# A two-layer decoder trunk: the convolution's LayerNorm by products with a matrix of ones, and the recurrence's transposes as 64x128 row tiles behind other tiled matmuls

## The chip, the cores and the metric

The kernel runs on one core of a Trainium2 chip. The metric is the device time in microseconds (us) of one execution. The kernel before takes 1475.71 us (median of three runs, 1475.03 to 1475.87).

## What is computed

Two layers work on x (512 tokens, 1024 channels). One projection feeds four branches of width 512: an RWKV-7 recurrence, a latent attention, a gated depthwise convolution and a cross-attention into 256 memory tokens. Each branch is multiplied by its gate and projected to 1024 channels; the four are merged with sigmoid gates, projected once more and normalized.

```python
for l in range(DEPTH):                                   # DEPTH = 2
    h = x @ w_in[l]                                      # all branches' columns
    y_rwkv = _rwkv7_branch(...)                          # 8 heads x 64, state by delta rule
    y_mla  = _mla_branch(...)
    y_conv = _conformer_conv_branch(...)                 # GLU, conv of 31 taps, LayerNorm, swish
    y_mem  = _memory_xattn_branch(...)
    branches = jnp.stack([y_rwkv, y_mla, y_conv, y_mem], axis=2)
    proj  = jnp.einsum('bsnc,ncd->bsnd', branches, w_o_branch[l])
    gates = jax.nn.sigmoid(merge.reshape(B, S, N_BRANCH, D) + b_gate[l])
    x = _layer_norm(DEEPNORM_ALPHA * x + jnp.sum(gates * proj, axis=2) @ w_out[l], ...)
```

## The kernel before, in words

**Large products.** Activations lie with channels on partitions, 512 tokens in a row. Each float32 operand is split into a high and a low part, and a product is made of three matmuls (`mm3`). A projection of 128 channels (`project`: eight blocks of the depth, 24 matmuls of 512 columns) writes a tile `ps_...`; a merge (`merge_items`) makes two such gate tiles `ps_m` and two products `po` of 12 matmuls each with the branch's output projection.

**The order.** `Plan` writes one program order for all engines while the kernel is built. It keeps a clock for each engine with costs that are written in the code, takes the large products from a list of items (`stream`), and steps side tasks (generators, made with `spawn`) as soon as their data should be there. On TensorE it puts a task's matmuls between those of the large products, which so cover the time in which the other engines work on the task. `Plan.shape` charges a change of the array's form (128x128, or tiles of 64x64, 64x128, 128x64). The order is fixed when the program is built; on the chip every engine goes through its own rows in order and waits where data are missing.

**PSUM.** Two banks `pp` hold the large products, two banks `pa` are shared by all side tasks, and the recurrence has two tiles of two banks each (`pg`).

**The convolution.** `taps` adds up the 31 taps of each 128 channels into `cacc` (VectorE). When four are there, `conv_norm` (lines 1288 to 1325) normalizes over the 512 channels of each token. In the kernel before it turns the data on TensorE to have tokens on partitions (`ct`, four transposes for each of four token blocks), takes mean and variance there with `bn_stats`, and turns the result back (`cb`, sixteen more). It starts only when the merge of the cross-attention is complete (line 1290), and turns back only after half of that of the latent attention (line 1311).

**The recurrence.** `rwkv_unit` (lines 838 to 1247) treats two heads' blocks and 256 tokens at once in chunks of 64; a layer has four units. A unit's name ends in layer, first block and half: `_1_2_1` is the last unit of the second layer. In a unit stand in turn: the scores `g` (64x64 tiles, four on the array at once); the substitution, 16x16 triangles inverted on GpSimd with DMA on both sides; `x0` to `x2`, which extend the inverse; `va`; `gb`, the unit's transfer matrices; the chain over the chunks, `w` with the state `S` between its steps; and the output `yb`, which is normalized by head (`bn_stats`, `bn_aggr`, a power on GpSimd in `gr`, eight activations on ScalarE), turned by four transposes `ty` and added into `r`. In the last unit of a layer, `w` is three products with a full array (`Gd`). When a layer's four units are through, `r` times its gate is split (`yrg`), and the layer's last merge, the rows `po0`, can use it; its first two gate tiles, `ps_m00` and `ps_m01`, need no `r`.

The recurrence needs b, k and v with tokens on partitions. The kernel before makes them in `tokens` (lines 1002 to 1013): four full 128x128 transposes `tk0` for b and four `tk1` for k, after the bonus product `bo`, and four `tk2` for v in a task of its own. Each takes one bank of `pa`.

## Time and profile before

| | |
|---|---|
| median of three runs | 1475.71 us |
| the profiled execution: span | 1473.7 us (the runs' median is 2.0 us over it; the time around the span) |
| mean granted TensorE clock | 0.999 |
| TensorE matmul, busy | 1463.7 us, 99% |
| VectorE, busy | 1032.8 us, 70% |
| ScalarE, busy | 681.5 us, 46% |
| GpSimd, busy | 148.3 us, 10% |

In the profile PE is TensorE, DVE VectorE, ACT ScalarE, POOL GpSimd and SP the engine that issues the DMAs. A timeline row has the start in us, the time from its start to the end of the last of its instructions in us, engine, line, operation, the tile written and those read, and how many instructions it stands for; the bracket at its end has the idle time before it and what ended that. A float32 matmul that is no transpose shows as two records. Matmuls overlap, so that the distance from start to start says what one costs.

### The profile page before, as it was taken

The page shows a single profiled execution, that of the slowest core. Times are in us where ns is not written, and L with a number is a line of the kernel's source. Part 1 is how long each engine was busy: PE and PEld are TensorE (multiplying, and loading weights), DVE is VectorE, ACT ScalarE, POOL GpSimd, SP SyncE. Part 2 cuts the span into 40 slices and gives each one's busy share as a digit, 9 for nine tenths or more (in the row PEclk, how much of TensorE's full clock was granted, in tenths as well). Part 3 has the DMA queues.
Part 4 walks back from the last instruction along what each step waited for, and adds up shares of the span by engine and source line. Part 5 has one row for each costly group of instructions (what it writes and reads, how often), then busy time and mean ns, then how long its engine had stood idle before and what let it go on. Part 6 is the DMA issues. An engine that isn't in the chain of part 4 may idle for free.

```text
span 1473.7 us, 28870 instructions
## 1 busy us (share of the span) xinstructions
PE 1463.7 (99%) x11729; PEld 1233.6 (84%) x11729; DVE 1032.8 (70%) x2017; ACT 681.5 (46%) x1325; POOL 148.3 (10%) x339
## 2 busy tenths in 40 slices
PE   9999999999999999999999999999999999999997
PEld 9888888888888888888999888888888888888886
DVE  6799997765657665645554899987867476747756
ACT  5556654425354443443264465633454454444331
POOL 0000000030303030000010000000041203121003
PEclk9999999999999999999999999999999999999999
DMA  7454332232222323334354253333232323233522
GB/s 220 129 144 107 90 110 95 86 77 95 81 77 83 90 76 97 122 122 130 102 166 121 62 151 78 118 94 101 83 96 76 96 57 101 75 86 122 171 96 83
DMA packets 89157, 153.49 MB, mean 104 GB/s; under 512 B 41024, under 2 KB 47424, under 8 KB 89024
## 3 DMA queue, kind: packets, MB, share of 16 engines
q1 hardware_dynamic: 89024, 151.65, 34.9%
q8 instruction: 92, 1.51, 0.4%
q14 instruction: 41, 0.34, 0.1%
HBM read 134.32 MB, written 5.77 MB: 95 GB/s over the span
## 4 chain that ended last, share of the span: by engine, by line
PE 96%; ACT 1%; DMA 1%; DVE 1%; POOL 1%; issue 0%; SPq 0%; DVEq 0%; POOLq 0%
PE ps_m L353 23%; PE po L353 11%; PE pz L353 4%; PE ps_v L353 3%; PE ps_cg L353 3%; PE ps_rg L353 3%; PE ps_xg L353 3%; PE ps_xq L353 3%; PE ps_k L353 3%; PE ps_val L353 3%; PE ps_glu L353 3%; PE ps_r L353 3%; PE ps_mg L353 3%; PE ms L353 2%; PE pl L353 2%; PE x L353 2%
## 5 line engine op out<-in xcount | busy, mean ns | idle before, releaser
L259 DVE SCALAR_TENSOR_TENSOR cacc<-hpad,prm,cacc 128x512 f32<-128x512 f32 x240 | 179.0, 748 | 3.8
L259 ACT ACTIVATE tm<-ps_m,prm 128x512 f32<-128x512 f32 x64 | 44.1, 689 | 152.2 <-PE ps_m L353 149.5
L259 DVE SCALAR_TENSOR_TENSOR mt<-tm,po 128x512 f32<-128x512 f32 x48 | 33.0, 687 | 85.1 <-PE po L353 85.0
L259 POOL TENSOR_TENSOR tmpW<-ZT,W 64x14 f32<-64x14 f32 (+6 forms) x112 | 43.9, 392 | 8.0
L259 ACT ACTIVATE mP<-ms,nmm 128x128 f32<-128x128 f32 (+3 forms) x64 | 33.7, 530 | 20.9 <-DVE nmm L259 16.1
L259 POOL TENSOR_SCALAR ZT<-W 64x256 f32<-64x256 f32 x8 | 4.5, 564 | 361.8 <-DMA W<-scr 361.8
L259 POOL TENSOR_TENSOR ZT<-ZT,tmpW 64x14 f32<-64x14 f32 (+6 forms) x112 | 39.7, 354 | 8.8
L259 DVE TENSOR_TENSOR merged<-merged,mt 128x512 f32<-128x512 f32 x48 | 33.3, 694 | 1.6
L259 POOL MEMSET D<- 128x8 f32 x8 | 0.9, 112 | 328.9 <-PE ms L353 313.0
L259 DVE CUSTOM_DVE_ANT_0 ms<-ms,causal 128x128 f32<-128x128 f32 (+3 forms) x64 | 31.1, 498 | 0.6 <-PE ms L353 0.2
L259 ACT COPY mPT<-mt 128x128 f32<-128x128 f32 (+3 forms) x64 | 26.4, 428 | 5.3 <-PE mt L358 5.0
L259 POOL TENSOR_SCALAR lrs<-lmv 128x1 f32<-128x1 f32 x8 | 4.3, 532 | 231.8 <-DVE lmv L259 226.9
L358 PE MATMUL mt<-cst,mP 128*128 128x128 f32 x160 | 26.8, 274 | 0.4 <-ACT mPT L259 0.4
L259 DVE TENSOR_SCALAR mP<-mP,smm 128x128 f32<-128x128 f32 (+3 forms) x64 | 24.8, 387 | 2.4
L259 DVE SCALAR_TENSOR_TENSOR merged<-tm,po 128x512 f32<-128x512 f32 x16 | 11.0, 687 | 22.0 <-PE po L353 19.9
L358 PEld LDWEIGHTS mt<-cst,mP 128*128 128x128 f32 x160 | 20.2, 140 | 6.8 <-issue 0.9
L259 ACT ACTIVATE yb<-yb,mr,gr 128x64 f32<-128x64 f32 x64 | 22.1, 430 | 1.4 <-DVE mr L259 1.4
L353 PE MATMUL ms<-kTl,qT 96*128 96x128 f32 (+3 forms) x64 | 21.5, 337 | 0.0
L259 POOL TENSOR_SCALAR gr<-gm 128x8 f32<-128x8 f32 x8 | 1.9, 242 | 191.3 <-DVE gm L259 191.3
L353 PE MATMUL ms<-kTh,qTl 96*128 96x128 f32 (+3 forms) x64 | 20.6, 323 | 0.0
L353 PE MATMUL ms<-kTh,qT 96*128 96x128 f32 (+3 forms) x64 | 20.6, 322 | 0.0
L259 ACT ACTIVATE xP<-xs,nmx 128x256 f32<-128x256 f32 x32 | 15.2, 475 | 11.2 <-DVE nmx L259 11.1
(3574 smaller groups left out, 5224.8 us busy)
## 6 DMA issues: line engine op xcount, KB each, us to landing
w<-in_w_ch_dram SPq DMA_DIRECT2D x146, 512.0 KB, 3.7
w<-in_w_o_dram SPq DMA_DIRECT2D x32, 512.0 KB, 3.6
w<-in_w_out_dram SPq DMA_DIRECT2D x16, 512.0 KB, 3.5
w<-in_w_lat_dram SPq DMA_DIRECT2D x15, 336.0 KB, 3.0
w<-in_w_mk_dram SPq DMA_DIRECT2D x8, 512.0 KB, 3.6
w<-in_w_mv_dram SPq DMA_DIRECT2D x8, 512.0 KB, 3.7
w<-in_w_qk_dram SPq DMA_DIRECT2D x8, 320.0 KB, 3.1
mr<-in_memT_dram SPq DMA_DIRECT2D x8, 256.0 KB, 5.6
```

The costliest lines, as they stand in the source:

```text
L259: return self.plan.keep(f(*a, **k))
L353: plan.keep(nc.tensor.matmul(o, lhsT, rhs, start=start, stop=stop))
L358: plan.keep(nc.tensor.transpose(o, i, ident))
```

## The change

**The convolution's norm.** The transposes go. The four `cacc` are added on GpSimd, the sum is split in two, and two matmuls with a 128x128 matrix of ones (`cs`) put the sum over all channels on every partition; the mean is subtracted from `cacc` in place. Squares (ScalarE) are added in the same way and summed by two matmuls (`cq`). One row of this goes by DMA to DRAM and comes back with 512 tokens as 128x4, the power is taken on GpSimd, and two further DMAs bring the result to all partitions. The two conditions on the merges go.

**The transposes of b, k and v.** A transpose is now made of 64 rows by 128 channels (`TQ`, a 64x128 row tile), with the upper and the lower half in different banks, so that two `pa` banks are taken at once. Those of b and k (16) stand directly behind `g`, those of v (8) directly behind the matmuls of `x0`. The inner order of the last group of `x0` changes with it (`for cp, h, c2 in quads`), and a few tiles take other places in SBUF.

```diff
+    def TQ(o, i, one):
+        plan.shape(64, 128)
+        plan.op("PE", 28.0, _names(o), _names(i))
+        plan.keep(nc.tensor.transpose(o, i, one))
...
+            def turned_by(ps, c, src):
+
+                for s in SUB:
+                    for cp in range(2):
+                        for h in range(2):
+                            e = c + 128 * s + 64 * cp
+                            TQ(ps[h][:, e:e + 64], src[s][HALF[h], 128 * cp:128 * cp + 128], one[h])
...
+            tk = yield from pa.take([128, 512], "tk0" + t, 2, None)
+            turned_by(tk, 0, [bt[:, s] for s in SUB])
+            turned_by(tk, 256, [kt[:, s] for s in SUB])
...
-                        TR(ps[:, 256 * s + 128 * cp:256 * s + 128 * cp + 128], src[s][:, 128 * cp:128 * cp + 128])
...
+            tv = yield from pa.take([128, 512], "tk2" + t, 2, None)
...
-                for cp, c2, h in quads:
+                for cp, h, c2 in quads:
                     MM(y0[HALF[h ^ cp], 1, s, h, c2], AR[HALF[h], s, 2 * cp + c2, 0], one[h], start=True, stop=True, four=True)
+            turned_by(tv, 0, vr)
...
-            yield lambda: added[3] == 8
-            for tb in range(4):
...
-                    TR(ps[:, 128 * i:128 * i + 128], cacc[i][:, 128 * tb:128 * tb + 128])
...
-                    TR(ps[:, 128 * tb:128 * tb + 128], ntok[tb][:, 128 * i:128 * i + 128])
...
+            MM(ps, all_ones, lo, start=True, stop=False)
+            MM(ps, all_ones, h, start=False, stop=True)
...
+                V.scalar_tensor_tensor(out=cacc[i], in0=ps, scalar=-1.0 / 512, in1=cacc[i], op0=ALU.mult, op1=ALU.add)
...
+            DMA(d4, row)
...
+            DMA(v4, d4.rearrange("o (p a) -> (o p) a", p=128))
...
+            DMA(d.rearrange("o (p a) -> (o p) a", p=128), v4)
...
+            DMA(rstd, d.to_broadcast([128, 512]))
```

**What moves on TensorE.** With other costs and conditions, `Plan` writes another order. Two places in the last unit of the second layer are shown; a row has the line, the operation, the tile written and those read (names end in layer, unit and a serial number), the size, and how often it stands there. The first place is the chain over the chunks (`w0` to `w2`, with `ps_rg` a projection for the recurrence's gate and `ty_1_2_0` the transposes of the unit before). Before:

```order
L353 MATMUL w0_1_2_1_15086<-S3_1_2_0_14861,Gd0_1_2_1_14850 128x64
L353 MATMUL w0_1_2_1_15086<-S3_1_2_0_14861,Gd1_1_2_1_14851 128x64
L353 MATMUL ps_rg1_1_15074<-xl2_1_8395,w215h_14792 128x512
L353 MATMUL ps_rg1_1_15074<-xh2_1_8394,w215h_14792 128x512
L353 MATMUL ps_rg1_1_15074<-xh2_1_8394,w215l_14793 128x512
L353 MATMUL ps_rg1_1_15074<-xl3_1_8400,w215h_14792 128x512
L353 MATMUL ps_rg1_1_15074<-xh3_1_8399,w215h_14792 128x512
L353 MATMUL ps_rg1_1_15074<-xh3_1_8399,w215l_14793 128x512
L353 MATMUL w1_1_2_1_15109<-S0_1_2_1_15089,Gd0_1_2_1_14850 128x64
L353 MATMUL w1_1_2_1_15109<-S0_1_2_1_15089,Gd1_1_2_1_14851 128x64
```

After:

```order
L353 MATMUL w0_1_2_1_15339<-S3_1_2_0_15178,Gd0_1_2_1_15132 128x64
L353 MATMUL w0_1_2_1_15339<-S3_1_2_0_15178,Gd1_1_2_1_15133 128x64
L353 MATMUL w1_1_2_1_15354<-S0_1_2_1_15351,Gd0_1_2_1_15132 128x64
L353 MATMUL w1_1_2_1_15354<-S0_1_2_1_15351,Gd1_1_2_1_15133 128x64
L358 MATMUL ty_1_2_0_15348<-cst_81,yb_1_2_0_15212 128x128 x4
L353 MATMUL w2_1_2_1_15360<-S1_1_2_1_15357,Gd0_1_2_1_15132 128x64
L353 MATMUL w2_1_2_1_15360<-S1_1_2_1_15357,Gd1_1_2_1_15133 128x64
L353 MATMUL yb_1_2_1_15374<-S3_1_2_0_15178,B_1_2_1_15323 64x64 x2
L353 MATMUL yb_1_2_1_15374<-S0_1_2_1_15351,B_1_2_1_15323 64x64 x2
```

The projection's rows between the steps are gone; `w1`, the transposes of the unit before, `w2` and `yb` follow each other directly.

The second place is the unit's last transposes `ty_1_2_1`; `ps_m00` is the first gate tile of the layer's last merge, `po00` that merge's first product, and `yrg0` to `yrg3` are the recurrence's gated result. Before:

```order
L353 MATMUL ps_m00_1_15276<-xl3_1_8400,w218h_15150 128x512
L353 MATMUL ps_m00_1_15276<-xh3_1_8399,w218h_15150 128x512
L353 MATMUL ps_m00_1_15276<-xh3_1_8399,w218l_15151 128x512
L358 MATMUL ty_1_2_1_15268<-cst_81,yb_1_2_1_15179 128x128 x4
L353 MATMUL ps_m00_1_15276<-xl4_1_8422,w218h_15150 128x512
L353 MATMUL ps_m00_1_15276<-xh4_1_8421,w218h_15150 128x512
L353 MATMUL ps_m00_1_15276<-xh4_1_8421,w218l_15151 128x512
```

After:

```order
L353 MATMUL yb_1_2_1_15374<-S2_1_2_1_15369,B_1_2_1_15323 64x64 x2
L358 MATMUL ty_1_2_1_15425<-cst_81,yb_1_2_1_15391 128x128 x4
L353 MATMUL po00_1_15469<-yrg0l_1_14797,w220h_14927 128x512
L353 MATMUL po00_1_15469<-yrg0h_1_14796,w220h_14927 128x512
L353 MATMUL po00_1_15469<-yrg0h_1_14796,w220l_14928 128x512
L353 MATMUL po00_1_15469<-yrg1l_1_14841,w220h_14927 128x512
L353 MATMUL po00_1_15469<-yrg1h_1_14840,w220h_14927 128x512
L353 MATMUL po00_1_15469<-yrg1h_1_14840,w220l_14928 128x512
L353 MATMUL po00_1_15469<-yrg2l_1_15462,w220h_14927 128x512
```

Before, the rest of `ps_m00` stands behind `ty_1_2_1`, and the 24 rows of `ps_m01` behind that. Now the product `po00`, which reads `yrg`, follows at once. Between the first row of `gb_1_2_1` and `po00` stood 135 matmuls of 512 columns (the last 15 of `ps_rg0`, all of `ps_rg1` to `ps_rg3`, `ps_m00` and `ps_m01`); now there is none. The same rows now stand ahead of `yb_1_2_0`. In the first layer `ty_0_2_1` had 87 such rows behind it ahead of `po00` and now has 12.

Over the whole order of TensorE the array changes from 128x128 to 64x64 or 64x128 tiles and back 57 times instead of 51; 16 of these visits now have a part in 64x128 form, 15 of them behind a part in 64x64.

## Prediction

> **What bounds the kernel now.** I read the engines' shares first, then the chain that ended last, then TensorE's timeline where the order changes.

> ```profile
> PE 1463.7 (99%) x11729; PEld 1233.6 (84%) x11729; DVE 1032.8 (70%) x2017; ACT 681.5 (46%) x1325; POOL 148.3 (10%) x339
> ...
> PE 96%; ACT 1%; DMA 1%; DVE 1%; POOL 1%; issue 0%; SPq 0%; DVEq 0%; POOLq 0%
> ```

> TensorE (PE) is busy for 1463.7 of 1473.7 us and makes up 96% of the chain. So the end moves by what TensorE's own rows cost, start to start, and by every wait that TensorE has to sit out. The kernel has almost none of these now, because its order always has large products to put between the steps of the side tasks. The change touches both, and I take them in turn.

> **What TensorE's rows cost.** The timeline of the last unit of the second layer, TensorE alone, has every kind of row that I need:

> ```profile
> 1330.72 0.67 PE L353 MATMUL gb<-BP,VA 64*64 64x128 f32 x16
> 1331.21 0.29 PE L353 MATMUL gb<-vt,bk 64*64 64x64 f32 x8
> 1331.33 0.30 PE L353 MATMUL gb<-VA,BP 64*64 64x64 f32 x8
> ...
> 1333.39 0.30 PE L353 MATMUL gb_1x<-VA,BP 64*64 64x64 f32 x8
> 1333.62 0.50 PE L353 MATMUL ps_rg<-xl,w214h 128*128 128x512 f32 x1
> ...
> 1338.52 0.55 PE L353 MATMUL w<-S,Gd 128*128 128x64 f32 x4
> ...
> 1342.61 0.39 PE L353 MATMUL ps_rg<-xh,w215l 128*128 128x512 f32 x1
> 1342.84 0.60 PE L358 MATMUL ty<-cst,yb 128*128 128x128 f32 x4
> 1343.28 0.56 PE L353 MATMUL w<-S,Gd 128*128 128x64 f32 x4
> 1343.64 0.48 PE L353 MATMUL ps_rg<-xl,w215h 128*128 128x512 f32 x1
> 1343.96 0.40 PE L353 MATMUL ps_rg<-xh,w215h 128*128 128x512 f32 x1
> ...
> 1345.58 0.40 PE L353 MATMUL ps_rg<-xh,w216l 128*128 128x512 f32 x1
> 1345.91 0.69 PE L353 MATMUL yb<-S,B 64*64 64x64 f32 x32
> 1346.53 0.50 PE L353 MATMUL ps_rg<-xl,w216h 128*128 128x512 f32 x1
> 1346.87 0.40 PE L353 MATMUL ps_rg<-xh,w216h 128*128 128x512 f32 x1
> ```

> A 512-column matmul takes 0.23 us (1342.61 to 1342.84), four full transposes 0.44 (1342.84 to 1343.28), so 0.11 each. The four `w` records with a full array take 0.36, and the row behind them stretches from 0.23 to 0.32: 0.45 in all, again 0.11 each, though only 64 columns pass through. What they share with the transposes is the load of 128 stationary columns, so I read 0.11 us as the price of that load. In 64x64 form eight records take 0.12 us (1331.21 to 1331.33), 0.015 each with four tiles at once, so about 0.06 on one tile. A visit to small tiles costs extra at its ends: 0.33 instead of 0.23 going in (1345.58), the 32 records at 0.015 leave 0.14 of 0.62 unexplained, and the first full row takes 0.34 instead of 0.23; together 0.35.

> **The convolution.** The transposes that go:

> ```profile
> L358 PE MATMUL tk<-cst,v 128*128 128x128 f32 x32 | 5.1, 281 | 0.0
> L358 PE MATMUL cb<-cst,cn 128*128 128x128 f32 x32 | 4.9, 276 | 0.0
> L358 PE MATMUL tk<-cst,bt 128*128 128x128 f32 x32 | 4.9, 274 | 0.0
> ...
> L358 PE MATMUL ct<-cst,cacc 128*128 128x128 f32 x32 | 4.8, 274 | 0.0
> L358 PE MATMUL tk<-cst,kt 128*128 128x128 f32 x32 | 4.8, 272 | 0.0
> ```

> 64 transposes (`ct`, `cb`) at 0.11 are 7.0 us; eight matmuls of 512 columns with ones come, at 0.23: 1.8. Net -5.2 us, all on the path. On ScalarE, VectorE and GpSimd, evictions and statistics are exchanged for squares, sums and scalings of the same 512 columns; on SP four DMAs per layer come, in one queue with the weights. I cost all that at nothing: in the new order over 1000 rows of TensorE stand between the sum of squares and the first product that reads the result, in either layer. If an SP wait held up a weight load, it would show as TensorE idle within a projection.

> **The transposes of b, k and v.** 96 full transposes go: 96 x 0.11 = 10.6 us. 192 half-height ones come. Their price isn't in the trace. Each loads 128 stationary columns and passes 64. If the load decides, a pair (upper and lower half at once) takes 0.11, one 0.055. If the passing columns decide, as on a 64x64 tile at 0.06, a pair takes 0.06, one 0.03. If the halves didn't overlap at all, one takes 0.11. I take 0.055, since `w` with a full array is the nearest row: 192 x 0.055 = 10.6, net 0. The bounds are -5 and +10.

> [...]

> **Changes of form.** Six visits to small tiles more: 6 x 0.35 = 2.1 us. Sixteen visits now hold a second form; nothing in the trace changes between two small forms. Bounds are 0 and the whole 0.35; I take 0.1, the price of going in: 1.6. The new inner order of `x0`'s last group puts two products in a row on one tile: between 0 and, if they then run one by one, 0.23 per unit (half as long again for 32 records at 0.015), 1.8 over eight units; I take 0, since four records of two products run side by side in either order.

> **The wait at the end of the second layer.** This is the largest term. Nothing is left to put between the last unit's steps, so TensorE sits out the chain. It follows from rows of the same unit, on the other engines:

> ```profile
> 1332.63 0.39 DVE L259 TENSOR_TENSOR H<-gb,dl 128x256 f32<-128x256 f32 x1
> ...
> 1334.16 0.85 DVE L259 TENSOR_TENSOR Gd<-gb_1x,cst 64x256 f32<-64x256 f32 x2
> ...
> 1339.11 0.48 DVE L259 SCALAR_TENSOR_TENSOR S<-w,dl,H 128x64 f32<-128x64 f32 x2 [0.36 <-PE w L353]
> ...
> 1346.38 1.22 DVE L259 TENSOR_TENSOR w218l<-w,w218h 128x1024 fp32r<-128x1024 f32 x1
> 1347.52 0.75 DVE L259 TENSOR_TENSOR yb<-yb,Y 128x256 f32<-128x256 f32 x2
> ...
> 1348.84 1.10 DVE L259 BATCH_NORM_STATS2 gs<-yb 128x6 f32<-128x64 f32 x8
> 1349.86 0.62 DVE L259 BATCH_NORM_AGGREGATE gm<-gs 128x2 f32<-128x6 f32 x8
> ...
> 1353.65 0.16 DVE L259 SCALAR_TENSOR_TENSOR mr<-gm,gr 128x8 f32<-128x8 f32 x1
> ...
> 1359.55 1.12 DVE L259 SCALAR_TENSOR_TENSOR r<-ty,prm,r 128x128 f32<-128x128 f32 x4 [0.20 <-PE ty L358]
> 1360.59 1.40 DVE L259 SCALAR_TENSOR_TENSOR r<-r,prm,rg 128x512 f32<-128x512 f32 x2
> ...
> 1365.18 0.68 DVE L259 TENSOR_TENSOR yrg2l<-r,yrg2h 128x512 fp32r<-128x512 f32 x1
> ```

> ```profile
> 1353.91 2.76 ACT L259 ACTIVATE yb<-yb,mr,gr 128x64 f32<-128x64 f32 x8 [1.43 <-DVE mr L259]
> ...
> 1363.90 0.62 ACT L259 CAST yrg2h<-r 128x512 fp32r<-128x512 f32 x1
> ```

> ```profile
> 1350.58 0.55 POOL L259 TENSOR_SCALAR gr<-gm 128x8 f32<-128x8 f32 x1 [15.78 <-DVE gm L259]
> 1351.21 1.64 POOL L259 TENSOR_TENSOR gr<-gr,mhalf 128x8 f32<-128x8 f32 x1
> ```

> I count from the start of `yb_1_2_0`, with 0.1 for each hop between engines (1350.48 to 1350.58). Its matmuls take 0.7, the two additions that free its bank 0.75; `gb_1_2_1` starts at 1.6 and takes 2.9. VectorE does the statistics (1.64, to 3.2), a weight split that stands there in the new order (1.2, to 4.4), then `H` to `Gd` (1332.63 to 1335.01, 2.4, to 6.8). `w0` starts at 6.9; its state is due 0.6 later, but VectorE has two more additions like `H` (0.8) and `mr` (0.16) in its queue and ends the state at 8.3. `w1` and its state (0.6 + 0.5) end at 9.5. Next in TensorE's queue is `ty_1_2_0`, behind the eight activations (from 8.0, 2.8): 10.8. `w2` follows at 11.2, its state is there at 12.5 after half of the `r` row. `yb_1_2_1` starts at 12.6 (0.7), additions to 14.1, statistics to 15.8, GpSimd (1350.58 to 1352.85, 2.3) to 18.2, `mr` and hops to 18.5, activations to 21.2, the last transpose and hop to 21.9, `r` to 23.0 and times its gate to 24.4, high part to 25.1, low part to 25.8. Then the last three matmuls of `po00` go, to 26.6.

> TensorE's own rows in that time cost 0.62 + 2.9 + 3 x 0.36 + 2 x 0.44 + 0.62 + 12 x 0.23 = 8.9 us, switches included. So 17.7 us of idle time come in, where there is none now. My chain assumes that nothing else stands in an engine's way; a price 15% off moves it by 4, and more could join in. In the first layer the 12 rows behind `ty_0_2_1` and the first half of `po00` (18 x 0.23 = 4.1) nearly cover the 4.6 us from there to the last low part: +0.5.

> **The clock.** At the kernel's end the trace shows what idling does to it:

> ```profile
> 1464.00:1466.00 2.00, 1.95 (x17) 1.75 (x15) 1.56 (x6) 0.60 (x1) 0.93 (x1) 1.00 0.17 59
> ...
> 1470.00:1474.00 4.00, 0.00 (x0) 0.00 (x0) 0.46 (x2) 0.00 (x0) 0.00 (x0) 0.53 0.36 131
> ```

> TensorE stops at 1465.95; a mean granted clock of 0.53 over the last 4 us is half the clock from 1470.2 on, 4.3 us later. Between `yb_1_2_1` and `ty_1_2_1` TensorE would idle for 8 us, so it would come back at half clock. When the full clock returns this row doesn't tell: +0 if within the half of `po00` that waits anyway, +2.5 if 5 us of needed work run at half. I take +1.

> [...]

> **The sum.** -5.2 + 0 + 2.1 + 1.6 + 17.7 + 0.5 + 1.0 = +17.7 us on the profiled execution, 1473.7 to 1491.4 us of span. With the 2.0 us by which the median stands above that span: 1493.4 us.

> **The rivals.** *Fast turning*: the passing columns set the price of a half-height transpose. For it speaks that the load hides on a 64x64 tile; against it the `w` rows. 192 x 0.03 = 5.8 instead of 10.6: 1488.5 us.

> *More waits*: a unit now needs both `pa` banks at once, 16 times, and behind the transposes in TensorE's queue stand the large products. If each waits 0.5 us for an eviction of about that length, +8: 1501.4 us. For it: the banks are shared with all side tasks. Against it: `Plan` puts the transposes where it reckons the banks free.

> *Faster, the rows alone decide*: the idle time at the layer's end stays out, because the chain runs in 9 us where I have 26.6. Then -5.2 + 0 + 3.7 = -1.5, and with fast turning -6.3: 1469.4 us. It decides from an idle time under 3.3 us. Each step's data dependence in the new order speaks against it: one GpSimd power and two rounds of activations already take 7.8 us.

> *No change*: as the last, with the load's price; 1474.2 us.

> **How the numbers follow.** Forecast 0.45, fast turning 0.27, more waits 0.2, faster 0.05, no change 0.03. The low end of the range takes the fast turning with an idle time 6 us shorter and no clock term: 1481.5. The high end is the rival with more waits and the 1.8 us of `x0`'s new inner order: 1503.2. About 0.2% (3 us) can be told from no change: faster by more 0.05, within it 0.03, slower by more 0.92.

> **What would show it.** In the profile after, TensorE idles about 18 us between `yb_1_2_0` and `po01` of the second layer, most of it ended by the activations of `yb` and by `S`, and almost nothing elsewhere; the granted clock dips there. Sixteen transposes behind `g` take 0.9 us start to start if the load decides, 0.5 if not. Four `cs` and four `cq` matmuls at 0.23. I am wrong if TensorE's idle time stays near 10 us in all, or if long idle times stand at `tk`, `g` or `x`.

## The result, and the profile after

The changed kernel takes 1500.5 us (median of four runs, 1497.6 to 1501.5) against 1475.4 us before (four runs, measured beside it): 1.0166 times the time, 95% interval 1.0154 to 1.0178. The forecast was 1493.4 us, slower, with a range that ends at 1503.2. The profiled execution is the fastest of the four, 1497.6 us with a span of 1495.9, so it holds 22.2 us of the loss. The other three show a lower granted clock (0.989 to 0.991 against its 0.992); by that they ran an estimated 3 to 9 us more at half clock, which fits the difference.

The page of the changed kernel: engines, the clock in 40 slices, and the chain that ended last.

```profile
PE 1466.4 (98%) x11769; PEld 1230.6 (82%) x11769; DVE 1039.2 (69%) x2013; ACT 684.8 (46%) x1379; POOL 161.3 (11%) x339
...
PEclk9999999999999999999999999999999999998999
...
PE 91%; DVE 3%; POOL 2%; DMA 2%; ACT 1%; issue 1%; SPq 0%; DVEq 0%; POOLq 0%; ACTq 0%
```

TensorE's share of the chain fell from 96% to 91%, and one slice near the end has a lower clock. The slice is the last unit of the second layer. Here is TensorE's timeline from `yb_1_2_0` on (start, duration, then the row; in brackets the idle time ahead and what ended it).

```profile
1366.72 0.27 PE L353 MATMUL yb<-causal,B 64*64 64x64 f32 x2
...
1367.23 0.62 PE L353 MATMUL gb<-BP,VA 64*64 64x128 f32 x16
...
1372.16 0.41 PE L353 MATMUL w<-S,Gd 128*128 128x64 f32 x2 [2.02 <-DVE Gd L259]
...
1373.38 0.66 PE L353 MATMUL w<-S,Gd 128*128 128x64 f32 x2 [0.81 <-DVE Gd L259]
...
1374.48 1.12 PE L353 MATMUL w<-S,Gd 128*128 128x64 f32 x4 [0.43 <-DVE S L259]
...
1375.39 0.90 PE L358 MATMUL ty<-cst,yb 128*128 128x128 f32 x2
...
1378.29 1.35 PE L353 MATMUL yb<-S,B 64*64 64x64 f32 x32
...
1385.20 0.48 PE L358 MATMUL ty<-cst,yb 128*128 128x128 f32 x1 [5.55 <-ACT yb L259]
...
1387.31 0.77 PE L353 MATMUL po<-yrg0l,w220h 128*128 128x512 f32 x1
...
1387.88 0.63 PE L353 MATMUL po<-yrg0h,w220h 128*128 128x512 f32 x1
1388.31 0.63 PE L353 MATMUL po<-yrg0h,w220l 128*128 128x512 f32 x1
...
1390.91 0.50 PE L353 MATMUL po<-yrg2l,w220h 128*128 128x512 f32 x1 [0.69 <-DVE yrg2l L259]
...
1392.42 0.39 PE L353 MATMUL po<-yrg0l,w220h 128*128 128x512 f32 x1
```

`yb_1_2_0` starts at 1366.72 and `po01` at 1392.42: 25.7 us. The longest wait, 5.55 us, is ended by ScalarE's activations of `yb`, as forecast. All idle time in this stretch makes 10.4 us: 6.5 ended by `yb`, 2.8 by `Gd`, 0.4 by `S` and 0.7 by `yrg2l`. The first `po` rows stand 0.43 us apart (1387.88 to 1388.31) in place of 0.23: half clock. The windows of the same kernel give the clock around both layers' ends (window, its length, busy time of PE, PEld, DVE, ACT and POOL, then the mean granted clock, the DMA share and GB/s).

```profile
636.00:640.00 4.00, 1.73 (x7) 1.11 (x6) 2.43 (x3) 1.76 (x3) 0.00 (x0) 0.93 0.49 165
640.00:644.00 4.00, 4.00 (x13) 3.14 (x12) 1.38 (x2) 0.62 (x1) 0.00 (x0) 0.65 0.18 73
644.00:648.00 4.00, 4.00 (x19) 3.32 (x18) 3.30 (x5) 2.94 (x5) 0.00 (x0) 1.00 0.02 4
...
1370.00:1374.00 4.00, 1.17 (x16) 0.81 (x6) 3.88 (x9) 0.74 (x2) 2.62 (x2) 0.91 0.71 181
1374.00:1378.00 4.00, 3.19 (x13) 2.27 (x12) 1.44 (x8) 2.76 (x8) 0.00 (x0) 0.50 0.89 334
...
1390.00:1394.00 4.00, 3.31 (x14) 2.52 (x14) 2.85 (x5) 0.75 (x2) 0.00 (x0) 0.96 0.00 0
```

A mean of 0.93 over 4 us is 0.56 us at half clock, 0.65 is 2.8: 3.4 us in the first layer. In the second it lasts from 1373.3 (0.91 is 0.7 us of four) to 1390.3, 17 us.

**The bookkeeping.** I take the stretch from the last `va` to the end of `po00` and subtract 0.226 us for each 512-column matmul in it, so that kernels with more or fewer of them there compare. What is left is 8.5 us before and 24.5 after in the second layer, 8.1 and 11.3 in the first: 16.0 + 3.1 us of the 22.2. Four waits elsewhere, counted start to start above a normal row, make about 6.6: ahead of `bo` (1.8), `cq` (1.6) and `x2` (1.5), and inside `gb` (1.6). (At the program's start TensorE also idles longer than before, but by 13.6 us both kernels are level again.) The convolution's rows give 6.5 back for the 64 transposes and take 1.9 for the eight sums: -4.6. All rows of `tk` together went from 8.9 to 8.3 us start to start, -0.6, the way out of each visit included. The sum is +20.5, and 1.7 us are left. About 1.0 of them is the half clock of the first layer: 2.1 of its 3.4 us lie behind `po00`, outside the stretch, where five rows take 0.43 us in place of 0.226. The last 0.7 I can't place; the ends of the six visits more, which aren't counted apart, belong to it.

### The profile page after: what moved, and what is told of

Its sections match the earlier page's. It is cut to its first block, busy times and chain, and to the rows that moved or that the text cites. A ratio compares the mean times of both kernels' runs of the same rounds, so it can differ in the third digit from the quotient of the medians.

```text
span 1495.9 us, 29023 instructions
## 1 busy us (share of the span) xinstructions
PE 1466.4 (98%) x11769; PEld 1230.6 (82%) x11769; DVE 1039.2 (69%) x2013; ACT 684.8 (46%) x1379; POOL 161.3 (11%) x339
## 3 DMA queue, kind: packets, MB, share of 16 engines
q8 instruction: 92, 1.51, 0.4%
## 4 chain that ended last, share of the span: by engine, by line
PE 91%; DVE 3%; POOL 2%; DMA 2%; ACT 1%; issue 1%; SPq 0%; DVEq 0%; POOLq 0%; ACTq 0%
PE ps_m L353 22%; PE po L353 11%; PE pz L353 4%; PE ps_rg L353 3%; PE ps_cg L353 3%; PE ps_xg L353 3%; PE ps_xq L353 3%; PE ps_val L353 3%; PE ps_glu L353 3%; PE ps_k L353 3%; PE ps_r L353 3%; PE ps_v L353 3%; PE ps_mg L353 2%; PE ms L353 2%; PE pl L353 2%; PE x L353 2%
## 5 line engine op out<-in xcount | busy, mean ns | idle before, releaser
L259 DVE SCALAR_TENSOR_TENSOR cacc<-hpad,prm,cacc 128x512 f32<-128x512 f32 x240 | 180.1, 753 | 3.8
L259 ACT ACTIVATE tm<-ps_m,prm 128x512 f32<-128x512 f32 x64 | 44.1, 689 | 147.7 <-PE ps_m L353 147.4
L259 DVE SCALAR_TENSOR_TENSOR mt<-tm,po 128x512 f32<-128x512 f32 x48 | 32.9, 686 | 78.6 <-PE po L353 78.6
L259 POOL TENSOR_TENSOR tmpW<-ZT,W 64x14 f32<-64x14 f32 (+6 forms) x112 | 47.8, 427 | 7.7
L259 ACT ACTIVATE mP<-ms,nmm 128x128 f32<-128x128 f32 (+3 forms) x64 | 33.7, 529 | 20.9 <-DVE nmm L259 16.1
L259 POOL TENSOR_TENSOR ZT<-ZT,tmpW 64x14 f32<-64x14 f32 (+6 forms) x112 | 40.2, 359 | 8.8
L259 POOL MEMSET D<- 128x8 f32 x8 | 0.9, 114 | 322.1 <-PE ms L353 313.5
L259 DVE TENSOR_TENSOR merged<-merged,mt 128x512 f32<-128x512 f32 x48 | 33.2, 692 | 1.7
L259 DVE CUSTOM_DVE_ANT_0 ms<-ms,causal 128x128 f32<-128x128 f32 (+3 forms) x64 | 31.1, 498 | 0.6 <-PE ms L353 0.2
L259 POOL TENSOR_SCALAR ZT<-W 64x256 f32<-64x256 f32 x8 | 6.7, 837 | 220.9 <-DMA W<-scr 220.9
L259 ACT COPY mPT<-mt 128x128 f32<-128x128 f32 (+3 forms) x64 | 26.4, 428 | 5.2 <-PE mt L358 5.0
L358 PE MATMUL mt<-cst,mP 128*128 128x128 f32 x160 | 26.8, 274 | 0.4 <-ACT mPT L259 0.4
L259 POOL TENSOR_SCALAR lrs<-lmv 128x1 f32<-128x1 f32 x8 | 4.3, 538 | 208.8 <-DVE lmv L259 204.0
L259 DVE TENSOR_SCALAR mP<-mP,smm 128x128 f32<-128x128 f32 (+3 forms) x64 | 24.8, 387 | 2.4
L259 ACT ACTIVATE yb<-yb,mr,gr 128x64 f32<-128x64 f32 x64 | 22.1, 430 | 9.3 <-DVE mr L259 9.3
L358 PEld LDWEIGHTS mt<-cst,mP 128*128 128x128 f32 x160 | 20.2, 140 | 6.8 <-issue 0.8
L259 POOL TENSOR_TENSOR csum<-csum,cacc 128x512 f32<-128x512 f32 x4 | 6.0, 1506 | 171.4 <-DVE cacc L259 171.4
L259 POOL TENSOR_SCALAR gr<-gm 128x8 f32<-128x8 f32 x8 | 3.2, 400 | 196.1 <-DVE gm L259 196.1
L353 PE MATMUL ms<-kTl,qT 96*128 96x128 f32 (+3 forms) x64 | 21.5, 337 | 0.0
L353 PE MATMUL ms<-kTh,qTl 96*128 96x128 f32 (+3 forms) x64 | 20.6, 322 | 0.0
L259 DVE SCALAR_TENSOR_TENSOR r<-ty,prm,r 128x128 f32<-128x128 f32 x32 | 9.5, 343 | 16.0 <-PE ty L358 16.0
L353 PE MATMUL ms<-kTh,qT 96*128 96x128 f32 (+3 forms) x64 | 20.6, 321 | 0.0
```

The lines of the kernel that those rows point to most:

```text
L259: return self.plan.keep(f(*a, **k))
L353: plan.keep(nc.tensor.matmul(o, lhsT, rhs, start=start, stop=stop))
L358: plan.keep(nc.tensor.transpose(o, i, ident))
```

## Theories and experiments

**My theory**: the new order has too few large rows left for the two layers' ends; the recurrence's transposes themselves cost no more than before. The convolution's rows are cheaper too, but its new work on ScalarE, VectorE and GpSimd makes TensorE wait in the first unit of each layer. **Rivals**: the half-height transposes or the pairs of banks cost the time wherever they stand; the convolution moves the large rows; its DMAs hold up the weights.

### 1. The convolution alone

The edit takes `conv_norm`, `over_channels` and `all_ones` from the changed kernel and leaves `rwkv_unit` as it is in the kernel before.

> The new convolution alone; the recurrence is that of the kernel before. In its order 114 large rows stand between va and the last ty of the second layer, as in the kernel before (12 in the changed kernel). My theory: the idle time at the end of the second layer belongs to the recurrence's part, and the waits of 1.7 us before bo and 1.5 us before cq belong to the convolution's work on ScalarE, VectorE and GpSimd. So this kernel gains the 5.2 us of rows, loses about 3 to those waits, and idles no more than 1 us at the layer's end: 1473 us against 1475.4, 1470.5 to 1475.5. Rival, the convolution is free beside TensorE (as I forecast): 1470. Rival, the convolution's later result moves the large rows: 1485 or more, with idle time at the end of the second layer.

Measured: 1473.0 us, ratio 0.9984 (0.9975 to 0.9993). The stretch at the second layer's end has 162 large rows and 8.5 us beside them, as before. So the convolution doesn't move the large rows away, and of the 5.2 us forecast it keeps 2.4. TensorE idles 0.62 us ahead of `bo`, 0.47 ahead of `cq`, 0.59 ahead of `x1` and 1.34 within it. The longest of these is no wait for the other engines' work (experiment 6).

### 2. The convolution with b and k

```diff
-            tv = yield from pa.take([128, 512], "tk2" + t, 2, None)
...
-            turned_by(tv, 0, vr)
...
-                tokens(tv, 0, vt)
+                vt.extend((yield from tokens1(2, vr, lambda: place("bt", "vt"))))   # four full transposes, one bank
```

> The changed kernel with v transposed as before (four full transposes in a visit of their own place, one pa bank); b and k stay half-height transposes behind g, with both pa banks at once. In its order 81 large rows stand between va and the last ty of the second layer. My theory: the pair of banks that x0 has to wait for with v is what made the recurrence late, so here the idle time at the end of the second layer is under 4 us in place of 17; rows gain 5.2 + about 1.5, the side engines' waits cost about 5: 1475 us, 1471 to 1480. Rival, any step that takes both banks makes the recurrence late: 1488 or more, idle over 10 us there.

Measured: 1484.9 us, ratio 1.0060 (1.0044 to 1.0077). The sign is right, the size isn't: 15.6 us of the loss go, but not 25. TensorE around the last `ty`:

```profile
1371.37 0.33 PE L358 MATMUL ty<-cst,yb 128*128 128x128 f32 x1 [3.97 <-ACT yb L259]
...
1373.48 0.77 PE L353 MATMUL po<-yrg0l,w220h 128*128 128x512 f32 x1
1374.06 0.63 PE L353 MATMUL po<-yrg0h,w220h 128*128 128x512 f32 x1
...
1377.08 0.79 PE L353 MATMUL po<-yrg2l,w220h 128*128 128x512 f32 x1 [0.69 <-DVE yrg2l L259]
```

The idle time is 5.4 us in the stretch, where I expected under 4. Behind the longest wait the clock goes to half for 10.2 us. `po` follows `ty` at once, at 0.43 us a row. I had left the clock out. The stretch holds 17.7 us beside its 93 large rows, 9.2 more than before.

### 3. The convolution with v

```diff
-            tk = yield from pa.take([128, 512], "tk0" + t, 2, None)
-            turned_by(tk, 0, [bt[:, s] for s in SUB])
-            turned_by(tk, 256, [kt[:, s] for s in SUB])
...
+            yield from tokens1(0, [bt[:, s] for s in SUB], lambda: [x[:, :, 0:64] for x in BP])   # full, one bank,
+            bk1 = yield from tokens1(1, [kt[:, s] for s in SUB], lambda: place("kt", "bk1"))      # in the old place
```

> The changed kernel with b and k transposed as before (full transposes, one bank each, in the old place); v stays as half-height transposes behind x0, with both pa banks. In its order 12 large rows stand between va and the last ty of the second layer, as in the changed kernel. My theory: v's pair of banks takes the large rows away, so the idle time of about 17 us stays: 1500 us, 1495 to 1505. Rival, the pair taken at g matters as much: about 1485, with half the idle time.

Measured: 1497.1 us, ratio 1.0141 (1.0125 to 1.0156); 25.7 us beside 24 large rows in the stretch. So v, placed directly behind `x0` with both banks taken there, is enough for nearly all of the loss. It isn't the only part that can bring it: b and k alone add 9.2 us at the same place (experiment 2), and the two don't add up. Whether the place or the pair of banks does it, this run doesn't separate.

### 11. The same instructions, another order

```diff
-            x0, y0 = yield from pg.take([128, 2, 512], "x0" + t, 2, soon)
             tv = yield from pa.take([128, 512], "tk2" + t, 2, None)
+            x0, y0 = yield from pg.take([128, 2, 512], "x0" + t, 2, soon)
```

> The changed kernel with two lines exchanged: the two pa banks for v are asked for ahead of x0's banks, not behind them. Instructions and buffers are the same; only the order moves. In it 36 large rows stand between va and the last ty of the second layer in place of 12, and 39 rather than 12 between the last ty and po00 of the first layer. My theory (the time hangs on how many large rows are left for these places): 24 rows x 0.225 = 5.4 us less idle time in the second layer, and the first layer's wait with its half clock goes, 2.3 + 1.7: 1491 us, 1488 to 1496. If the idle time comes from the instructions themselves: 1500.5.

Measured: 1490.8 us, ratio 1.0104 (1.0090 to 1.0118). All instructions of the change are there, and 9.7 us of the loss go with two lines exchanged. In the traces 5.0 us of that show at the layers' ends: 2.4 us in the second layer's stretch (24.5 to 22.1, where I expected 5.4), 2.6 in the first (11.3 to 8.7). By the profiled executions the kernels are 6.7 us apart (1495.9 and 1489.2 us of span): that of the changed kernel is the fastest of its four. So the number of the expectation came out, but its larger part only by half: some of the agreement is luck. With the other kernels this gives a series for the second layer, from the traces (with the 12 rows of `po00`):

| kernel | large rows in the stretch | time beside them, us |
|---|---|---|
| before; 1 | 162; 162 | 8.5; 8.5 |
| 5 | 138 | 11.5 |
| 2 | 93 | 17.7 |
| 11 | 48 | 22.1 |
| changed; 3 | 24; 24 | 24.5; 25.7 |

From 162 to 93 rows a missing row costs 0.13 us, from 93 to 24 about 0.1: less than its own 0.226. That the rows' places matter too would explain it and isn't shown. In the first layer 162 or more rows leave 8.0 to 8.7 in these kernels, 135 to 138 leave 11.2 to 11.3. No run gives the changed kernel all its large rows back, so the series ties the time to the order without reaching the 8.5 us again.

### 5. b and k with more large rows left

```diff
-GATHER = 1500.0
+GATHER = 800.0
...
+            sqs = [u(f"csq{i}" + t_) for i in range(4)]   # squares first, then the additions
...
+                plan.due(t)                                # behind the tanh
+                yield
```

(on the kernel of experiment 2)

> The new convolution and half-height transposes of b and k, v as before, with three edits: the four squares have buffers of their own, so that ScalarE doesn't wait for GpSimd between them; the step behind the convolution's tanh is given to VectorE only when the tanh is due; small-tile visits are gathered over 0.8 us in place of 1.5. In its order 114 large rows stand between va and the last ty of the second layer, as in the kernel before. My theory (the loss is large rows that ran out, plus waits for ScalarE, VectorE and GpSimd; the rows themselves are cheaper): rows -5.2 for the convolution and 8 x (0.64 - 0.88) = -1.9 for b and k, about 2 us left of the waits, no idle time at the layer's end and no half clock: 1470.3 us, 1468 to 1473. Rival, the pairs of banks and the extra form cost time wherever they stand: 1475 or more.

Measured: 1479.9 us, ratio 1.0036 (1.0023 to 1.0049). My number failed by 10 us, and the rival's is nearer, but the trace shows waits, not rows. (The profiled execution took 1484.3 us, the longest of the five, so not all that it shows is in the median.) At the layer's end:

```profile
1373.31 0.39 PE L353 MATMUL po<-yrg1h,w220l 128*128 128x512 f32 x1
1375.97 0.50 PE L353 MATMUL po<-yrg2l,w220h 128*128 128x512 f32 x1 [2.27 <-DVE yrg2l L259]
1376.31 0.48 PE L353 MATMUL po<-yrg2h,w220h 128*128 128x512 f32 x1
1376.59 0.63 PE L353 MATMUL po<-yrg2h,w220l 128*128 128x512 f32 x1
```

The 12 rows behind the last `ty` and the first half of `po00` don't cover the chain through `r` to `yrg2l`, just as in the first layer of the changed kernel (2.27 us there too), and the clock falls to half behind it. Two more waits of 2.0 and 2.7 us stand in `x1` and `x2` of the first units, each with 3.4 us of half clock behind it. At the granted clock of 0.50 that the windows of the changed kernel show, 3.4 us do the work of an estimated 1.7.

### 6. The convolution alone, squares in buffers of their own

```diff
-            q, r = u("csq0" + t_), u("csq1" + t_)
...
+            sqs = [u(f"csq{i}" + t_) for i in range(4)]
...
+                plan.due(t)
+                yield
```

> The new convolution alone, as in the first experiment, with the four squares in buffers of their own and the step behind the tanh given to VectorE when the tanh is due. If the waits before bo (0.62 us) and x1 (0.59) of that experiment come from VectorE and ScalarE queues that the convolution holds up, they shrink: 1472 us, against 1473.0. If they come from the DMAs or the order, no change: 1473. The wait of 0.47 before cq stays in either case.

Measured: 1479.0 us, ratio 1.0019 (1.0011 to 1.0028): 6 us worse than experiment 1, against both expectations. `bo` waits as before (0.59), and a longer wait stands within `x1` of the first unit, with 3.4 us of half clock behind it. Its windows, us by us:

```profile
343.00:344.00 1.00, 0.60 (x43) 0.47 (x33) 0.03 (x1) 0.00 (x0) 0.00 (x0) 1.00 1.11 348
344.00:345.00 1.00, 0.00 (x0) 0.00 (x0) 0.00 (x0) 0.00 (x0) 0.00 (x0) 1.00 0.80 303
345.00:346.00 1.00, 0.00 (x0) 0.00 (x0) 0.00 (x0) 0.00 (x0) 0.00 (x0) 1.00 0.16 57
346.00:347.00 1.00, 0.56 (x10) 0.44 (x10) 0.10 (x1) 0.00 (x0) 0.00 (x0) 0.80 0.04 16
```

For over 2 us no engine does anything, TensorE in the middle of a group of 32, and the profile knows no releaser ("issue"). Just ahead the DMA engines are full: SP had waited for the convolution's DMAs, then sent the broadcast of 256 KB and two weights of 512 KB in a row. The page lists DMA queues of their own for instructions. One of them, `q8`, brings a packet of 16 KB for every 256 records of TensorE (matmuls, weight loads and semaphore events; 92 packets, 23530 records). The twelve experiments and the changed kernel have 19 waits over 0.3 us that no other engine ends and that begin after the first matmul. Among them are the 1.34 in experiment 1 and the one in the changed kernel's `gb`. All 19 stand at the same place in this count, behind 193 or 194 records beyond a multiple of 256, and end 1.2 to 1.6 us after a packet has landed. Here it began at 343.99, when TensorE had been idle for 0.4 us, and landed at 344.93; TensorE went on at 346.44. In the kernel before the shortest time from a landing to the record at that place is 1.9 us. That TensorE waited here for the instructions in a late packet is my reading of these times; that the data ahead held the packet up fits the full DMA engines (a share of 1.11 from 343 to 344), but isn't shown.

### 9 and 10. No DMAs behind the sum of squares

The four DMAs and GpSimd's power go; in 9 on the kernel of experiment 1, in 10 on the changed kernel.

```diff
-            row = u("crow" + t_, 512, p=1)
...
-            DMA(rstd, d.to_broadcast([128, 512]))
+            V.tensor_scalar(out=rstd, in0=ps, scalar1=1.0 / 512, scalar2=LN_EPS, op0=ALU.mult, op1=ALU.add)
+            S.activation(rstd, rstd, AF.Sqrt)
+            V.reciprocal(rstd, rstd)
```

> The new convolution alone, as in the first experiment, but the four DMAs between the sum of squares and the scaling are gone: every partition of cq already holds the sum, so ScalarE takes the square root of all 128x512 elements and VectorE the reciprocal. In its order 114 large rows stand between va and the last ty of the second layer. My theory: a part of the waits beside the convolution comes from those DMAs, which hold SP's queue, so that the weights behind them come late and bunched with the broadcast of 256 KB (the 1.34 us of issue and the 0.59 in front of x1 in the first experiment): 1471 us, 1469 to 1473, against 1473.0. Rival, the waits come from the work on VectorE, ScalarE and GpSimd alone, of which this has more: 1473 or above.

> The changed kernel with the same edit: no DMAs between the sum of squares and the scaling. Its order is that of the changed kernel in all large rows. The waits of 1.41 before x2 and 1.33 inside gb in the second layer go if those DMAs cause them; the 1.68 before bo, the 1.48 before cq and the idle time at both layers' ends stay: 1498 us against 1500.5. If they are not from the DMAs: 1500.5.

Measured: the convolution alone 1475.4 us, ratio 0.9999 (0.9990 to 1.0008), so worse than with the DMAs (1473.0); the whole change 1497.6 us, ratio 1.0154 (1.0140 to 1.0168), where the interval overlaps that of the changed kernel, so the time of 10 tells nothing. In its trace the wait ahead of `x2` is gone, but 1.32 us stand ahead of `x0` instead, and 0.93 of the "issue" wait in `gb` are left. In 9 no "issue" wait is left in `x1`, which fits the DMAs as its cause; but experiments 3 and 4, which have the DMAs, show none either. Others took its place: TensorE idles 0.77 us ahead of `x0` and 0.83 ahead of `x1`. VectorE's two reciprocals and ScalarE's four table loads more (seven, where experiment 1 has three) are work that wasn't there:

```profile
L259 DVE RECIPROCAL crstd<-crstd 128x512 f32<-128x512 f32 x2 | 6.7, 3353 | 2.7 <-ACT crstd L259 2.7
L259 ACT ACT_TABLE_LOAD x7 | 9.0, 1283 | 2.2 <-DVE crstd L259 1.4 <-PEq L2230 0.7
```

So the waits are not the DMAs' alone. That the new work on VectorE and ScalarE makes those of 9 is likely, since these two engines end them, and not shown apart.

### 12. The convolution's additions on VectorE

```diff
-                    G.tensor_tensor(out=x, in0=x, in1=y, op=ALU.add)
+                    V.tensor_tensor(out=x, in0=x, in1=y, op=ALU.add)
-            G.tensor_tensor(out=s, in0=cacc[0], in1=cacc[1], op=ALU.add)
+            V.tensor_tensor(out=s, in0=cacc[0], in1=cacc[1], op=ALU.add)
```

(on the kernel of experiment 1)

> The new convolution alone, as in the first experiment, with the six additions of 128x512 elements per layer on VectorE (0.7 us each) in place of GpSimd (1.3 to 1.5 us each). In its order 114 large rows stand between va and the last ty of the second layer. My theory: GpSimd's additions delay the squares and the sums, make VectorE's neighbouring steps three times as long (2.0 in place of 0.7 us beside one) and so cause the waits before bo (0.62) and cq (0.47); with 0.3 us that each wait costs beside its idle time: 1471.5 us, 1470 to 1473, against 1473.0. Rival, VectorE's queue is the cause and gets longer by this: 1473 or above.

Measured: 1472.3 us, ratio 0.9977 (0.9968 to 0.9986), the fastest kernel of this study. Against 1 the gain is small (0.7 us, the intervals overlap), but the wait ahead of `bo` is gone from the trace, as expected. The one ahead of `cq` in the second layer isn't (0.74). What GpSimd's additions do is best seen in the changed kernel, ahead of its `bo`, on four engines:

```profile
317.88 2.03 DVE L259 TENSOR_TENSOR M<-M,cst 128x512 f32<-128x512 f32 x1
...
318.07 1.29 POOL L259 TENSOR_TENSOR csq<-csq,csq 128x512 f32<-128x512 f32 x1
...
319.39 0.63 ACT L259 ACTIVATE csq<-cacc 128x512 f32<-128x512 f32 x1 [3.15 <-POOL csq L259]
319.93 0.60 ACT L259 CAST rbh<-w 128x512 fp32r<-128x512 f32 x1
...
320.56 0.74 DVE L259 TENSOR_TENSOR rbl<-w,rbh 128x512 fp32r<-128x512 f32 x1 [0.65 <-ACT rbh L259]
```

```profile
321.45 0.48 PE L353 MATMUL bo<-rbl,bones 128*128 128x512 f32 x1 [1.68 <-DVE rbl L259]
```

Read backwards: TensorE waits 1.68 us for `rbl`, VectorE for `rbh`, and `rbh` stands on ScalarE behind a square that waits 3.15 us until GpSimd has added the one before. GpSimd meanwhile works on the substitution and adds in between. The squares and their additions are the convolution's, and the recurrence pays. In experiments 1 and 6 the same addition stands beside VectorE's two steps `w`, which `rbh` reads (2.20 and 2.19 us, against 0.95 in the changed kernel); that fits `bo` waiting in 6 as in 1, although the squares no longer wait for GpSimd there.

### 4 and 7. What a half-height transpose costs

```diff
-                for s in SUB:
-                    for cp in range(2):
-                        for h in range(2):
+                for h in range(2):
+                    for s in SUB:
+                        for cp in range(2):
```

> The changed kernel, with the four upper halves of each operand first and the four lower ones behind them, in place of upper and lower by turns; all else and the rest of the order is the same. If a half-height transpose costs 0.03 us because an upper and a lower one run side by side (58 ns a pair), the halves now run one by one at 0.058: 192 x 0.029 = 5.6 us more, 1506 us. If the price doesn't come from the pairing but from the 64 columns that pass, one by one at 0.03: 1500.5, no change. If the loads of 128 columns can't hide without a partner, 0.11 each: 192 x 0.08 = 15 us more, 1516.

```diff
                             TQ(ps[h][:, e:e + 64], src[s][HALF[h], 128 * cp:128 * cp + 128], one[h])
+                            if h == 0:
+                                plan.keep(nc.tensor.transpose(ps[h][:, e:e + 64], src[s][HALF[h], 128 * cp:128 * cp + 128], one[h]))
```

> The changed kernel with each upper half-height transpose issued twice, 96 rows more; the order is otherwise the same. The halves that I meant to keep apart still started in pairs in the fourth experiment, so it didn't tell what one costs on its tile. If one tile takes 0.058 us for each: 96 x 0.058 = 5.6 us more, 1506 us, and the 24 rows behind g take 0.95 from the first start to the last in place of 0.49. If the array takes any of them in 0.03: 2.8 more, 1503, and 0.72. If the load of 128 columns sets 0.11 for a tile: 10.3 more, 1511, and 1.7.

Measured: 1498.9 us for the halves apart, ratio 1.0155 (1.0140 to 1.0170), no change; 1506.7 us with the upper ones twice, ratio 1.0204 (1.0188 to 1.0219). The first number agrees with "the passing columns set it", but that is not what happened. The timeline of experiment 4, where four upper ones (`tk`) stand ahead of four lower ones (`tk_1x`) in the program:

```profile
1353.39 0.27 PE L363 MATMUL tk<-cst,v 64*128 64x64 f32 x1
1353.40 0.27 PE L363 MATMUL tk_1x<-cst,v 64*128 64x64 f32 x1
1353.50 0.22 PE L363 MATMUL tk<-cst,v 64*128 64x64 f32 x1
1353.51 0.22 PE L363 MATMUL tk_1x<-cst,v 64*128 64x64 f32 x1
1353.56 0.22 PE L363 MATMUL tk<-cst,v 64*128 64x64 f32 x1
1353.58 0.22 PE L363 MATMUL tk_1x<-cst,v 64*128 64x64 f32 x1
```

They start in pairs all the same, from the second on 0.06 us apart. The experiment didn't separate what it was to separate. Experiment 7 did: twice the upper ones, and 24 rows behind `g` take 0.99 us from the first start to the last, where 16 take 0.49. So a 64x128 tile takes one in 0.06, two tiles work side by side, and that is 0.03 each. The time rose by 6.2 us, where 96 x 0.058 = 5.6 were expected.

### 8. Spare rows in the idle time

```diff
+            if diag and l:
+                spare = pp.pool.tile([128, 512], F32, tag="pp", name="spare" + t)
+                for i in range(14):     # 44 behind yb
+                    plan.keep(nc.tensor.matmul(spare[:, 0:256], ones[0], ones[1], start=True, stop=True))
```

> The changed kernel with spare matmuls of 256 bf16 columns that nothing reads: 14 behind the last gb of the second layer (1.5 us) and 44 behind its last yb (4.9 us), where TensorE idles 2.0 and 5.6 us. The waits stay; only the clock can differ. If the half clock there (17.1 us of records) costs what the rows in it say (w, ty, yb and nine po rows at twice their price, about 3.5 us), the time falls to 1497. If it costs the 1 us that I forecast: 1499.5. If the spare rows stand in the chain's way: above 1501.

Measured: 1498.5 us, ratio 1.0153 (1.0139 to 1.0167), between the two numbers, and the interval overlaps that of the changed kernel. The spare rows took the idle time in the stretch from 10.4 to 5.0 us and the half clock from 17.1 to 10.2, but the stretch is no shorter (24.9 us beside its large rows, 24.5 without them). The rows tell why:

```profile
1366.03 0.27 PE L353 MATMUL yb<-causal,B 64*64 64x64 f32 x2
...
1387.83 0.40 PE L353 MATMUL po<-yrg1h,w220l 128*128 128x512 f32 x1
1390.08 0.50 PE L353 MATMUL po<-yrg2l,w220h 128*128 128x512 f32 x1 [1.86 <-DVE yrg2l L259]
...
1392.12 0.63 PE L353 MATMUL po<-yrg0l,w220h 128*128 128x512 f32 x1
```

Here `ty_1_2_1` and the first half of `po00` ran at full clock. Still the row that reads `yrg2l` starts 24.05 us after `yb_1_2_0`, where the changed kernel needs 24.19: TensorE only waits longer for it, 1.86 us in place of 0.69. So the half clock on these rows costs 0.14 us. The longer wait in turn brought half clock to the last rows of `po00`, which take 2.04 us in place of 1.51. Between `w1` and `yb_1_2_1` both kernels run at half clock, so that part of the price isn't separated.

## Why the prediction was right, and where it was not

- **The wait at the end of the second layer** was the reason, and right in size. Forecast: 26.6 us from `yb_1_2_0` to the end of `po00`, own rows 8.9, so 17.7. Measured: 25.7, and 16.0 us more than before in the stretch. The steps, forecast and measured from the same start: `w0` 6.9 and 5.4, `w2` 11.2 and 10.7, `yb_1_2_1` 12.6 and 11.6, end of the activations 21.2 and 20.4, `po01` 26.6 and 25.7. `w0` was early because its first half needs only the first `Gd`; `w2` gained less, since it stands behind `ty_1_2_0`, whose activations end at 10.4 (forecast 10.8). The sign that I had named, about 18 us of idle time there, shows as 10.4: the chain has the forecast length, but TensorE's own rows fill 15.3 us of it in place of 8.9, most of them at half clock. Elsewhere 10.5 us are idle, where I had named almost nothing. Experiments 2, 3 and 11 tie the time to the order.
- **The clock** was put at +1 us with a fall 4.3 us after TensorE stops. Here it fell at 1373.3, when two waits had left TensorE idle for 2.7 of the last 3.4 us, and stayed down for 17 us. Where the forecast looked for its price, at `ty_1_2_1` and the first half of `po00`, it is 0.14 us (experiment 8): of the two values weighed there, 0 was nearly right. But the fall came earlier than forecast, and so `yb_1_2_1` takes 1.35 us in place of the 0.69 of the rows before, with VectorE waiting for it. Both together make an estimated 0.8 us, so the +1 comes out nearly right by another way.
- **The first layer's end**, forecast +0.5, cost 3.1: mis-sized. I counted 4.6 us from `ty_0_2_1` to the last low part. From the end of `ty` at 632.26 it took 6.3 to the end of `yrg2l` at 638.58, for which TensorE waited, and 6.9 to that of the last low part, because two weight splits (1.22 and 1.23 us) stood between the same steps on VectorE:

```profile
633.34 1.22 DVE L259 TENSOR_TENSOR w102l<-w,w102h 128x1024 fp32r<-128x1024 f32 x1
634.47 1.41 DVE L259 SCALAR_TENSOR_TENSOR r<-r,prm,rg 128x512 f32<-128x512 f32 x2
636.76 1.23 DVE L259 TENSOR_TENSOR w103l<-w,w103h 128x1024 fp32r<-128x1024 f32 x1 [0.88 <-ACT w103h L259]
637.90 0.68 DVE L259 TENSOR_TENSOR yrg2l<-r,yrg2h 128x512 fp32r<-128x512 f32 x1
```

  The 2.27 us of idle time brought 3.4 us of half clock, which I had not foreseen here. That was bad luck: the same wait in experiments 3, 4 and 8 brought none (see the last section). Experiment 5 shows the same wait in the second layer.
- **The convolution's rows**, forecast -5.2, measured -4.6. The step that failed is "I cost all that at nothing" for the other engines. Large rows do cover the way from the sum of squares to its reader; what I didn't look at is who else stands in ScalarE's and VectorE's queues behind the new steps: `rbh` and `rbl` for `bo`, `PP` for `x2`. Experiment 1 kept 2.4 of the 5.2.
- **The half-height transposes**, taken at 0.055 us each by the load of 128 columns, cost 0.03: the rival of fast turning was right on the price. One tile turned out a transpose with 128 loaded columns every 0.06 us (experiment 7), so the 0.11 us that I read off the `w` rows as the price of such a load was no bound here. Why, no run here shows.
- **The changes of form**: 57 visits in place of 51, as forecast. The second form adds 0.16 us behind `g` (its visit, with the rows at both ends, went from 2.63 to 3.27 us, of which 16 x 0.03 = 0.48) and none behind `x0` (2.95 to 3.18 us, 8 x 0.03 = 0.24); I took 0.1. The new inner order of `x0` costs 0.03 us a unit (2.92 to 2.95, experiments 1 and 2): the value 0 was right.
- **More waits** came, 6.6 us against the 8 of that rival, but not from its cause: no wait over 0.3 us stands ahead of a `tk` row. Those ahead of `bo` and `cq` stand, smaller, in experiment 1 too, where no bank is taken in pairs. The one in `gb` ends 1.6 us after an instruction packet has landed (experiment 6). What the pairs of banks did is at least in part in the order (experiment 11): they made the units later against the large rows.

Against my sum of +17.7 us the profiled execution has -2.7 at the second layer's end (the clock's 1.0 counted in), +2.6 at the first, +0.6 for the convolution's rows, -4.3 for transposes and visits (-0.6 in place of +3.7), +6.6 of waits and the 1.7 left over, half clock for the most part: +22.2. The median lies 3 us above that execution's time. So the forecast was 7.1 us low, inside its range. The main term and its mechanism were right; that the sum of the others came so near is in part luck, since 7.0 us of errors down stand against 11.5 up.

## What to carry to other kernels

Where a serial chain is hidden by filler, count the filler that the new order leaves for its last steps: here instructions that were no dearer by themselves cost 16 us in one place, because 138 large rows had moved ahead of the last unit. Work moved from the bounding engine to others that are half idle isn't free where something for the bounding engine stands behind it in their queues: of 5.2 us of rows 2.4 were left here (experiment 1). Ask for the resource that is hard to get first, not while holding another one that others need: two lines exchanged gave 9.7 us here (experiment 11).

## What the runs showed of the hardware

```profile
315.94 0.78 DVE L259 TENSOR_TENSOR M<-M,cst 128x512 f32<-128x512 f32 x1
316.70 0.71 DVE L259 TENSOR_TENSOR rbl<-w,rbh 128x512 fp32r<-128x512 f32 x1
```

  The two times added make 0.78 + 1.29 = 2.07, nearly the 2.03. By the records VectorE's step begins first (317.88 against 318.07), so the order of the starts doesn't tell which of the two was kept waiting. Why the times add up, no run here shows. GpSimd's steps are longer too: one of 64x56 elements takes 1.19 us at 316.05, beside VectorE's weight split of 1.22 us, and one of the same size 0.29 just ahead of it.
